# Seven block products for eight in the gate and up projections of a float32 encoder layer

## The chip, the cores and the metric

The kernel runs on one core of one Trainium2 chip. The metric is the device time of one execution in microseconds (us), from the start of the program to its end. TensorE (PE in the profile) multiplies, VectorE (DVE) and ScalarE (ACT) do the elementwise work, SyncE (SP) issues the transfers, and each engine works through its own queue in order.

## The reference

One layer of an encoder on 512 tokens of 1024 features, float32, in four sublayers, each with an RMSNorm before and after it:

```python
def swiglu(x, w_gate, w_up, w_down):
    return (jax.nn.silu(x @ w_gate) * (x @ w_up)) @ w_down

f = swiglu(rms_norm(h, ffn1_pre_g[i]), ffn1_w_gate[i], ffn1_w_up[i], ffn1_w_down[i])
h = h + 0.5 * rms_norm(f, ffn1_post_g[i])
m = hybrid_mixer(rms_norm(h, mix_pre_g[i]), ...)
h = h + rms_norm(m, mix_post_g[i])
f = swiglu(rms_norm(h, ffn2_pre_g[i]), ffn2_w_gate[i], ffn2_w_up[i], ffn2_w_down[i])
h = h + 0.5 * rms_norm(f, ffn2_post_g[i])
e = (p[i] @ ple_w_proj[i]) * jax.nn.sigmoid(rms_norm(h, ple_pre_g[i]) @ ple_w_gate[i])
h = h + rms_norm(e, ple_post_g[i])
```

`w_gate` and `w_up` are 1024 x 2816, `w_down` is 2816 x 1024, so each of the two feed-forward sublayers (FFN) has 22 tiles of 128 hidden features.

## The kernel before

Features lie on the 128 partitions and tokens along the free axis. An activation of 1024 features is eight tiles `[128, 512]`. Each product is made in float32r from values split in two parts (high and low), by three matmuls: `mm3` (L227) multiplies weight-high by x-high (L228), weight-high by x-low (L229) and weight-low by x-high (L230). The weights are the stationary side, the tokens the moving side, so one matmul has a 128x128 weight tile and 512 columns (256 where the tokens are taken in halves).

The weights come as a stream of chunks `[128, 1024]` of 512 KB (class `Stream`, L167). `load` issues a chunk's transfer from SP into one of `NRAW` = 2 buffers `raw`. `pump` splits it: ACT writes the high part `whi` (L195), DVE subtracts and writes the low part `wlo` (L196, seen as L160, the helper `tt`). There are `NB` = 8 buffers of each, and `free` pumps `SPLIT_AHEAD` = 4 chunks ahead of the one that was used up.

In an FFN the 11 groups of hidden tiles (two gate tiles and two up tiles each) stand in three parts, groups 0 to 2, 3 to 6 and 7 to 10. `group` (L344) makes one group from four chunks: 8 input tiles x 4 output tiles x 3 = 96 matmuls of 512 columns into four PSUM banks. The evacuation `ev_gu` (L418) multiplies the gate by the tokens' norm factor `rb`, applies SiLU on ACT, multiplies by the up product and splits the result into `zh` and `zl`. `rb` is left out of the up product: the factor that is missing in a token of f is taken care of by the norm after the FFN, with `scaled` (L272). After each part come the down products of its groups in two output halves.

The order of the instructions is made by emission: `Clock` (L65) advances with each product emitted, and tasks (norms, residual updates, splits) are emitted between products at distances given in the table `TIMES`; within that order the framework's scheduler places each engine's queue. At the end of a sublayer `last_group` (L369) takes the last products by halves of the tokens, `ahead` (L387) splits the chunks that the next sublayer begins with, as many as the `NB` buffers hold, and `boundary` (L395) does the norms, the residual and the next input's split. `first_group` (L352) then takes the next sublayer's first four chunks, by halves of the tokens.

Of the kernel before, what the change touches and what calls it, by code (L numbers as in the profile page):

```python
# [27 lines left out]
NB = 8  # L28
NRAW = 2
SPLIT_AHEAD = 4  # L30
# Where steps go between the products: distances on the emission clock, by sublayer boundary, head pair or channel group.
# [14 lines left out]
    "out": 3.8,  # L46
    "held": 2,
# [6 lines left out]
class Task:  # L54
    """Work emitted in steps: a generator that yields how long (us of products) to wait before its next step."""
# [7 lines left out]
class Clock:  # L63
    """Orders the emission: time advances with the products emitted, and due steps of tasks go between them."""
# [35 lines left out]
    def need(self, t, steps=None):  # L100
        """Emits what is left of a task, or of its first steps."""
# [13 lines left out]
def kernel(  # L115
# [13 lines left out]
    wraw = ctx.enter_context(tc.tile_pool(name="wraw", bufs=NRAW))  # L129
    wsp = ctx.enter_context(tc.tile_pool(name="wsp", bufs=NB))  # L130
# [35 lines left out]
    class Stream:  # L166
        def __init__(self):  # L167
            self.loaded = 0
            self.split = 0
            self.done = 0  # L170
            self.hold = False
            self.freed = set()
            self.raw = {}
            self.parts = {}

        def load(self, upto):
            while self.loaded < min(upto, n_chunks):
# [5 lines left out]
                self.loaded += 1  # L183

        def pump(self, upto):
            while self.split < min(upto, self.done + NB, n_chunks):
                c = self.split
                self.load(c + 1)
                raw = self.raw.pop(c)
# [3 lines left out]
                for i in range(0, CH, w):  # L193
                    sl = slice(i, i + w)
                    nc.scalar.copy(hi[:, sl], raw[:, sl])  # L195
                    tt(lo[:, sl], raw[:, sl], f32(hi[:, sl]), ALU.subtract)  # L196
                self.parts[c] = (hi, lo)
                self.split += 1
                self.load(self.split + NRAW)
# [54 lines left out]
    veps = act.tile([P, NT], F32, name="veps")  # L254
# [17 lines left out]
    def norm(sl, rc, wait, scaled=False):  # L272
# [11 lines left out]
        if scaled:  # L284
            for b in range(nb):
                nc.scalar.activation(sd[:, b:b + 1], ps[:, b:b + 1], AF.Sqrt, bias=veps[:, b0 + b:b0 + b + 1],
                                     scale=1.0 / D)
        else:
            nc.scalar.activation(sd[:, :nb], ps[:, :nb], AF.Sqrt, bias=eps, scale=1.0 / D)
        if rc is not None:  # L290
            nc.vector.tensor_scalar(veps[:, b0:b0 + nb], ps[:, :nb], EPS / D, EPS * EPS, op0=ALU.mult, op1=ALU.add)
# [16 lines left out]
    def emit_group(c0, nch, rhs, ps, sl, free, evac=None, before=None):  # L308
        """All output tiles together, k outermost; with evac, one output tile after the other."""
# [8 lines left out]
        if evac is None:  # L318
            for c in range(nch):
                for kk in range(2):  # L320
                    if before:
                        before(2 * c + kk)
                    for t in range(4):
                        one(c, kk, t)
                if free:
# [11 lines left out]
    def half_banks():  # L337
        """Four accumulators of 256 columns in two banks; the first product of a bank opens both."""
# [5 lines left out]
    def group(c0, nch, rhs, evac, late=()):  # L344
        ps = [bank("g") for _ in range(4)]
        emit_group(c0, nch, rhs, ps, slice(0, S), True)
# [5 lines left out]
    def first_group(c0, rhs, evac, chains):  # L352
        """The first products of a sublayer, by halves of the tokens, as its input comes."""
# [15 lines left out]
    def last_group(c0, nch, rhs, evac, chain):  # L369
        """The last products of a sublayer, by halves of the tokens; returns the tasks that follow each."""  # L370
# [16 lines left out]
    def ahead():  # L387
        """Splits of the chunks that the next sublayer begins with."""
        upto = min(ws.done + NB, n_chunks)
# [5 lines left out]
    def boundary(f, gpost, gnext, scaled):  # L395
        def chain(sl, i):
            yield from norm(sl, None, at("nb", i), scaled)
# [13 lines left out]
    def ffn(chains, gpost, gnext):  # L411
        f = [None] * KD
        late = ()
        for pi, (g0, g1) in enumerate(PARTS):
# [3 lines left out]
            def ev_gu(t, ps, sl, j0, held={}):  # L418
                if t % 2 == 0:
                    g = ttile("t")  # L420
                    tt(g[:, sl], ps, rb[:, sl], ALU.mult)
                    nc.scalar.activation(g[:, sl], g[:, sl], AF.Silu)  # L422
# [3 lines left out]
                if j not in zh:  # L426
                    zh[j], zl[j] = ztile(j)
                v = vtile("v")
                tt(v[:, sl], ps, g[:, sl], ALU.mult)
                nc.scalar.copy(zh[j][:, sl], v[:, sl])  # L430
# [554 lines left out]
```

## Time and profile before

| what | value |
|---|---|
| runs: median (lowest, highest) of 3 | 1114.62 us (1113.77, 1114.8) |
| profiled execution, first to last instruction | 1111.1 us |
| what lies around the span, by the median | 3.5 us |
| PE busy in the span | 1094.0 us (98%) |
| DVE busy, ACT busy | 578.6 us (52%), 454.1 us (41%) |
| traffic over the span | 96 GB/s |

A row of a view names the line in the kernel, the engine, the operation and the tiles: `wlo<-raw,whi` reads `raw` and `whi` and writes `wlo`. Matmuls overlap in the array, so the length of one in a row (0.39 us) is more than the distance between two starts; the distance is what counts.

### The profile page before, as it was taken

Reading aid. Unit: us, or ns where it says so; the run is one execution under the profiler, and the core shown is the slowest. Engines: PE = TensorE matmul, PEld = TensorE weight load, DVE = VectorE, ACT = ScalarE, POOL = GpSimd, SP = SyncE. Lnnn points to the kernel's source line nnn. Section 1 sums busy time; section 2 is a strip of 40 time slices with the busy share of each in tenths; the row PEclk is TensorE's granted clock in tenths of the full one; section 3 lists DMA queues with packets and bytes.
Section 4 is the critical chain, followed back from the end, with each engine's and each line's share of the span. In section 5 each row is a group of like instructions: output and inputs, shape, how many; then the busy total and the mean of one; then the engine's idle time right before and its main releaser. Section 6 shows DMA issues by size and latency. Waiting matters only on the chain.

```text
span 1111.1 us, 14120 instructions
## 1 busy us (share of the span) xinstructions
PE 1094.0 (98%) x5610; PEld 930.1 (84%) x5610; DVE 578.6 (52%) x1041; ACT 454.1 (41%) x765; POOL 0.7 (0%) x6
## 2 busy tenths in 40 slices
PE   9999999999999999999999999999999999999995
PEld 7888888888889988887888899888888888889994
DVE  6642334333434987977444439632334333434976
ACT  7533223212323665366232257523223212323784
POOL 0000000000000000000000000000000000000000
PEclk9999999999999999999999999999999999999998
DMA  6553222232332043231223210533232222332112
GB/s 221 184 162 118 95 95 95 95 94 95 97 97 73 20 133 114 76 95 59 95 95 95 95 58 31 176 117 96 95 95 95 94 95 95 97 99 72 38 58 76
DMA packets 37010, 107.94 MB, mean 97 GB/s; under 512 B 4816, under 2 KB 11472, under 8 KB 36944
## 3 DMA queue, kind: packets, MB, share of 16 engines
q1 hardware_dynamic: 36800, 107.01, 29.8%
q8 instruction: 44, 0.72, 0.3%
q14 instruction: 22, 0.18, 0.1%
q10 hardware_dynamic: 144, 0.03, 0.0%
HBM read 104.93 MB, written 2.10 MB: 96 GB/s over the span
## 4 chain that ended last, share of the span: by engine, by line
PE 94%; DVE 2%; ACT 2%; issue 1%; DMA 0%; SPq 0%; DVEq 0%; ACTq 0%
PE g L228 25%; PE g L230 25%; PE g L229 25%; PE gate L228 2%; PE gate L229 2%; PE gate L230 2%; PE br L228 1%; PE br L230 1%; PE br L229 1%; DVE o L160 1%; ACT e L567 1%; PE v L229 1%; PE xp L228 1%; PE v L228 1%; PE v L230 1%; PE xp L230 1%
## 5 line engine op out<-in xcount | busy, mean ns | idle before, releaser
L160 DVE TENSOR_TENSOR wlo<-raw,whi 128x1024 fp32r<-128x1024 f32 (+1 forms) x195 | 235.3, 1208 | 340.8 <-ACT whi L195 340.2
L195 ACT CAST whi<-raw 128x1024 fp32r<-128x1024 f32 (+1 forms) x195 | 202.1, 1038 | 422.6 <-PE g L229 301.1
L228 PE MATMUL g<-uh,whi 128*128 128x512 f32 (+1 forms) x960 | 345.9, 362 | 0.4 <-ACT whi L195 0.4
L229 PE MATMUL g<-ul,whi 128*128 128x512 f32 (+1 forms) x960 | 346.3, 361 | 0.0
L230 PE MATMUL g<-uh,wlo 128*128 128x512 f32 (+1 forms) x960 | 345.7, 361 | 0.5 <-DVE wlo L160 0.5
L230 PEld LDWEIGHTS g<-uh,wlo 128*128 128x128 f32 x960 | 180.7, 188 | 28.6 <-DVE wlo L160 0.9
L228 PEld LDWEIGHTS g<-uh,whi 128*128 128x128 f32 x960 | 180.7, 188 | 28.3 <-ACT whi L195 0.9
L229 PEld LDWEIGHTS g<-ul,whi 128*128 128x128 f32 x960 | 180.8, 188 | 27.5 <-DVE ul L163 0.2
L228 PE MATMUL g<-zh,whi 128*128 128x512 f32 (+1 forms) x512 | 179.9, 351 | 0.0
L230 PE MATMUL g<-zh,wlo 128*128 128x512 f32 (+1 forms) x512 | 179.0, 350 | 0.0
L229 PE MATMUL g<-zl,whi 128*128 128x512 f32 (+1 forms) x512 | 177.9, 347 | 0.0
L230 PEld LDWEIGHTS g<-zh,wlo 128*128 128x128 f32 x512 | 96.0, 188 | 14.1
L229 PEld LDWEIGHTS g<-zl,whi 128*128 128x128 f32 x512 | 96.1, 188 | 13.6
L228 PEld LDWEIGHTS g<-zh,whi 128*128 128x128 f32 x512 | 96.3, 188 | 12.1
L160 DVE TENSOR_TENSOR acc<-acc,sq 128x256 f32<-128x256 f32 (+1 forms) x96 | 44.7, 466 | 17.9 <-ACT sq L269 16.7
L422 ACT ACTIVATE t<-t 128x512 f32<-128x512 f32 (+1 forms) x46 | 27.9, 610 | 63.5 <-DVE t L160 63.4
L160 DVE TENSOR_TENSOR t<-g,rb 128x512 f32<-128x512 f32 (+1 forms) x46 | 30.5, 667 | 39.6 <-PE g L230 38.4
L228 PE MATMUL gate<-uh,whi 128*128 128x512 f32 x128 | 50.6, 395 | 0.0
L230 PE MATMUL gate<-uh,wlo 128*128 128x512 f32 x128 | 50.0, 390 | 0.0
L229 PE MATMUL gate<-ul,whi 128*128 128x512 f32 x128 | 49.9, 390 | 0.0
L430 ACT CAST zh<-v 128x512 fp32r<-128x512 f32 (+1 forms) x46 | 27.3, 596 | 27.9 <-DVE v L160 27.8
L160 DVE TENSOR_TENSOR zl<-v,zh 128x512 fp32r<-128x512 f32 (+1 forms) x46 | 30.5, 665 | 13.1 <-ACT zh L430 13.1
(150 smaller groups left out, 960.8 us busy)
## 6 DMA issues: line engine op xcount, KB each, us to landing
raw<-in_wst SPq DMA_DIRECT2D x191, 512.0 KB, 3.4
h<-in_x SPq DMA_DIRECT2D x8, 256.0 KB, 5.7
bm<-in_bias SPq DMA_DIRECT2D x64, 32.0 KB, 3.3
out<-o SPq DMA_DIRECT2D x16, 128.0 KB, 1.7
raw<-in_wst SPq DMA_DIRECT2D x4, 128.0 KB, 3.5
g_sb<-in_gains ACTq DMA_DIRECT2D x1, 34.0 KB, 3.0
edge_sb<-in_edge SPq DMA_DIRECT2D x1, 32.0 KB, 5.9
```

The costliest lines, as they stand in the source:

```text
L160: nc.vector.tensor_tensor(o, a, b, op=op)
L195: nc.scalar.copy(hi[:, sl], raw[:, sl])
L228: nc.tensor.matmul(o, wh, xh, start=first, stop=False, **kw)
L229: nc.tensor.matmul(o, wh, xl, start=False, stop=False, **kw)
L230: nc.tensor.matmul(o, wl, xh, start=False, stop=last, **kw)
L422: nc.scalar.activation(g[:, sl], g[:, sl], AF.Silu)
L430: nc.scalar.copy(zh[j][:, sl], v[:, sl])
L567: nc.scalar.activation(e[:, ii, :], e[:, ii, :], AF.Exp, bias=mn[:, ii:ii + 1], scale=-1.0, accum_out=sm[:, ii:ii + 1])
```

## The change

In each FFN the groups 3 to 10 (16 of the 22 pairs of tiles) are made by a scheme of seven block products in place of eight. A group is a product of two by two blocks: the outputs are halved into gate and up (two tiles each), the 1024 features into two halves, the tokens into two halves. Seven products of such blocks, some of sums of weight blocks with sums of input blocks, give the four output blocks. One product has 2 output tiles x 4 feature tiles x 3 = 24 matmuls of 256 columns, a group 168 in place of 96 of 512 columns. The seven are added up in three PSUM banks p, q, r; ACT copies three intermediate sums out (m1, m16, m7), and DVE makes three of the output blocks from these and a bank.

What goes with it:

- `Stream` has operations in place of chunks: four chunks of a fast group give seven splits. Four sums of weight blocks are made on DVE before (`both`, and in place in `raw`). `NRAW` is 5, `NB` is 6.
- The inputs have to be normalized before they are summed: `normalized` makes `un` = gain x h x rb, `renew` splits it into `uh`, `ul` again during group 1, `combined` makes the sums of blocks and splits them into eight pairs of tiles x. Groups 0 and 1 still use the input without `rb`, and their evacuation multiplies a second time by `rb`. The norm after the FFN loses `scaled`.
- The tiles x take buffers (tag `y`) of the mixer's bias tiles `bm`, so the 64 transfers of the bias wait until x has been used in the first FFN; before they stood among the first 40 us of weight loads and later ones.

```diff
-NB = 8
-NRAW = 2
+FAST = range(3, 11)
+NB = 6
+NRAW = 5
+RAW_AHEAD = 2
...
+        def source(self, n):
+            kind, c, i = self.ops[n]
+            if not kind:
+                return self.raw[c], (c,)
+            a21, a22, a11, a12 = (self.raw.get(c + j) for j in range(4))
+            if i == 2:
+                self.both = wsum.tile([P, CH], F32, tag="sum", name="both")
+                tt(self.both, a21, a22, ALU.add)
+                tt(a21, a21, a11, ALU.add)
+                tt(a11, a11, self.both, ALU.add)
+            if i == 6:
+                tt(a12, a12, a11, ALU.add)
...
+        def product(i, o, first):
+            wh, wl = ws.get(c0 + i)
+            for t in range(2):
+                for kk in range(4):
+                    w = slice((kk * 2 + t) * P, (kk * 2 + t + 1) * P)
+                    xh, xl = moving(i, kk)
+                    mm3(o[:, t * 256:(t + 1) * 256], wh[:, w], wl[:, w], xh, xl,
+                        first and kk == 0 and t == 0, kk == 3, skip_group_check=True)
+            ws.free(c0 + i)
...
+        product(0, p, True)
+        m1 = kept("m1", p)
+        product(1, q, True)
+        made(0, 0, q, m1, ALU.add)
+        product(2, p, False)
+        m16 = kept("m16", p, acc)
+        product(3, r, True)
+        m7 = kept("m7", r)
+        product(4, p, False)
+        made(1, 1, m7, p, ALU.subtract)
+        product(5, r, False)
+        made(1, 0, r, m16, ALU.subtract)
+        product(6, p, False)
+        done(0, 1, p, True)
...
+            def fast(gi):
+                j0 = 2 * (gi - g0)
+                v = {}
+                def block(row, column, c, banked):
+                    if row not in v:
+                        v[row] = vtile("v")
+                    g = ttile("g")[:, LEFT] if banked else c[:, LEFT]
+                    nc.scalar.activation(g, c[:, LEFT], AF.Silu)
+                    tt(v[row][:, HALVES[column]], c[:, RIGHT], g, ALU.mult)
+                    if (row, column) in ((1, 0), (0, 1)):
+                        split_z(j0 + row, v[row], slice(0, S))
+                fast_group(take(7), moving, block)
```

DVE's queue in the second FFN part of the first FFN, before, over group 4 of the kernel (`t`, `v` and `zl` are the evacuation, a number behind `wlo` is the chunk):

```order
L160 TENSOR_TENSOR wlo26_1045<-raw26_966,whi26_1044 128x1024
L160 TENSOR_TENSOR wlo27_1075<-raw27_996,whi27_1074 128x1024
L160 TENSOR_TENSOR wlo28_1105<-raw28_1048,whi28_1104 128x1024
L160 TENSOR_TENSOR t_998<-g_874,rb_105 128x512
L160 TENSOR_TENSOR t_1007<-g_876,rb_105 128x512
L160 TENSOR_TENSOR v_1003<-g_875,t_998 128x512
L160 TENSOR_TENSOR wlo29_1135<-raw29_1078,whi29_1134 128x1024
L160 TENSOR_TENSOR zl_1002<-v_1003,zh_1001 128x512
L160 TENSOR_TENSOR v_1012<-g_877,t_1007 128x512
L160 TENSOR_TENSOR zl_1011<-v_1012,zh_1010 128x512
```

The same engine and part now (`w` are output blocks made from a bank, `raw` and `both` on the left are weight sums, the number behind `wlo` is the split):

```order
L165 TENSOR_TENSOR raw26_1088<-raw26_1088,raw28_1322 128x1024
L165 TENSOR_TENSOR wlo31_1294<-raw25_1086,whi31_1293 128x1024
L165 TENSOR_TENSOR w_1263<-q_1203,m1_1233 128x512
L165 TENSOR_TENSOR wlo32_1325<-raw28_1322,whi32_1324 128x1024
L165 TENSOR_TENSOR v_1265<-w_1263 128x256
L165 TENSOR_TENSOR raw28_1322<-raw28_1322,both_1391 128x1024
L165 TENSOR_TENSOR wlo33_1359<-raw29_1328,whi33_1358 128x1024
L165 TENSOR_TENSOR raw29_1328<-raw29_1328,raw28_1322 128x1024
L165 TENSOR_TENSOR wlo34_1396<-raw28_1322,whi34_1395 128x1024
L165 TENSOR_TENSOR w_1362<-m7_1332,p_1202 128x512
L165 TENSOR_TENSOR wlo35_1432<-raw26_1088,whi35_1431 128x1024
L165 TENSOR_TENSOR v_1364<-w_1362 128x256
```

The evacuation no longer stands in one piece behind the group: its steps stand between the splits and the sums for the group after it.

ACT's queue at that place, before:

```order
L195 CAST whi28_1104<-raw28_1048 128x1024
L422 ACTIVATE t_998<-t_998 128x512
L195 CAST whi29_1134<-raw29_1078 128x1024
L422 ACTIVATE t_1007<-t_1007 128x512
L430 CAST zh_1001<-v_1003 128x512
L430 CAST zh_1010<-v_1012 128x512
L195 CAST whi30_1186<-raw30_1108 128x1024
```

And now, over the first five of the seven products of one group:

```order
L470 COPY m1_1233<-p_1202 128x512
L239 CAST whi32_1324<-raw28_1322 128x1024
L577 ACTIVATE w_1263<-w_1263 128x256
L239 CAST whi33_1358<-raw29_1328 128x1024
L470 COPY acc_107<-p_1202 128x512
L239 CAST whi34_1395<-raw28_1322 128x1024
L470 COPY m7_1332<-r_1204 128x512
L239 CAST whi35_1431<-raw26_1088 128x1024
```

Between two copies out of a bank now stands a cast for a later group, and once a SiLU that reads what DVE made.

PE's queue around the end of group 0 of the first FFN, before (`nsum` and `nb` are the sums and the broadcast of the norm):

```order
L303 MATMUL nb_318<-dh_300,ones_r_76 128x256
L281 MATMUL nsum_322<-ones_75,acc_104 128x1 x2
L229 MATMUL g_188<-ul6_102,whi3_178 128x512
L230 MATMUL g_188<-uh6_94,wlo3_179 128x512
...
L304 MATMUL nb_318<-dl_301,ones_r_76 128x256
L228 MATMUL g_186<-uh7_95,whi3_178 128x512
...
L303 MATMUL nb_344<-dh_329,ones_r_76 128x256
```

And now:

```order
L336 MATMUL nb_319<-dh_301,ones_r_79 128x256
L321 MATMUL nsum_323<-ones_78,acc_107 128x1 x2
L273 MATMUL g_191<-uh7_98,whi3_180 128x512
L274 MATMUL g_191<-ul7_106,whi3_180 128x512
L275 MATMUL g_191<-uh7_98,wlo3_181 128x512
L337 MATMUL nb_319<-dl_302,ones_r_79 128x256
L336 MATMUL nb_344<-dh_329,ones_r_79 128x256
L273 MATMUL g_394<-uh0_91,whi4_216 128x512
```

The six products that stood between the last `nb` matmul of the first token half and the first of the second half stand ahead of both now.

## Rows read from the trace of the kernel before

**Rows 1.** The page: busy time by engine, and the chain that ended last

```profile
PE 1094.0 (98%) x5610; PEld 930.1 (84%) x5610; DVE 578.6 (52%) x1041; ACT 454.1 (41%) x765; POOL 0.7 (0%) x6
...
PE 94%; DVE 2%; ACT 2%; issue 1%; DMA 0%; SPq 0%; DVEq 0%; ACTq 0%
```

**Rows 2.** Busy time by stretch: two FFN parts, a last group, a first group

```profile
core 0: us, PE busy (x) PEld busy (x) DVE busy (x) ACT busy (x) POOL busy (x), PEclk, DMA share, GB/s
105.64:192.73 87.09, 87.09 (x386) 72.07 (x384) 32.40 (x36) 24.90 (x32) 0.00 (x0) 1.00 0.30 97
...
903.38:990.47 87.09, 87.09 (x385) 72.07 (x384) 33.30 (x38) 24.40 (x30) 0.00 (x0) 1.00 0.30 97
...
345.77:369.03 23.26, 23.26 (x200) 23.19 (x198) 13.25 (x32) 9.97 (x22) 0.00 (x0) 1.00 0.07 24
...
670.16:695.54 25.38, 25.18 (x211) 24.94 (x209) 24.96 (x67) 19.23 (x47) 0.00 (x0) 1.00 0.13 43
```

**Rows 3.** Timeline of PE: start, length, instruction; 512 columns, then 256

```profile
60.20 0.39 PE L230 MATMUL g<-uh,wlo 128*128 128x512 f32 x1
60.42 0.39 PE L228 MATMUL g<-uh,whi 128*128 128x512 f32 x1
...
355.19 0.28 PE L230 MATMUL g<-zh,wlo 128*128 128x256 f32 x1
355.31 0.28 PE L228 MATMUL g<-zh,whi 128*128 128x256 f32 x1
...
381.69 0.28 PE L228 MATMUL g<-uh,whi 128*128 128x256 f32 x1
381.81 0.28 PE L229 MATMUL g<-ul,whi 128*128 128x256 f32 x1
```

**Rows 4.** Groups of DVE's instructions by form: busy, mean ns, idle before, releaser

```profile
L160 DVE TENSOR_TENSOR wlo<-raw,whi 128x1024 fp32r<-128x1024 f32 x191 | 233.7, 1224 | 340.7 <-ACT whi L195 340.2
...
L160 DVE TENSOR_TENSOR zl<-v,zh 128x512 fp32r<-128x512 f32 x42 | 28.9, 688 | 13.1 <-ACT zh L430 13.1
```

**Rows 5.** Timeline of DVE where instructions stand back to back

```profile
347.18 1.22 DVE L160 TENSOR_TENSOR wlo<-raw,whi 128x1024 fp32r<-128x1024 f32 x1
348.31 0.69 DVE L160 TENSOR_TENSOR acc<-acc,sq 128x512 f32<-128x512 f32 x1
348.91 0.42 DVE L160 TENSOR_TENSOR f<-g,f 128x256 f32<-128x256 f32 x1
349.25 0.68 DVE L160 TENSOR_TENSOR acc<-acc,sq 128x512 f32<-128x512 f32 x1
```

**Rows 6.** Groups of ACT's instructions by form

```profile
L195 ACT CAST whi<-raw 128x1024 fp32r<-128x1024 f32 x191 | 200.5, 1051 | 422.5 <-PE g L229 301.1 <-PE gate L229 42.9 <-PE br L229 28.0
...
L430 ACT CAST zh<-v 128x512 fp32r<-128x512 f32 x42 | 25.8, 614 | 27.9 <-DVE v L160 27.8
...
L455 ACT COPY f<-g 128x512 f32<-128x512 f32 x16 | 9.4, 585 | 11.1 <-PE g L230 10.3
...
L793 ACT ACTIVATE g<-g 128x256 f32<-128x256 f32 x16 | 6.4, 411 | 4.2 <-DVE g L160 4.2
```

**Rows 7.** The page, issues of transfers: count, KB each, us to landing

```profile
raw<-in_wst SPq DMA_DIRECT2D x191, 512.0 KB, 3.4
```

**Rows 8.** Timeline, ACT between the two norm broadcasts at the start

```profile
26.33 0.37 ACT L305 COPY rb<-nb 128x256 f32<-128x256 f32 x1 [0.19 <-PE nb L304]
26.59 0.70 ACT L299 ACTIVATE dh<-ident,rc_pre 128x128 fp32r<-128x128 f32 x2
```

**Rows 9.** Timeline, DVE and PE where first groups of a sublayer begin

```profile
374.77 0.16 DVE L294 RECIPROCAL rc<-sd 128x2 f32<-128x2 f32 x1
...
1047.45 0.28 PE L228 MATMUL g<-uh,whi 128*128 128x256 f32 x1
...
1050.97 0.48 DVE L163 SCALAR_TENSOR_TENSOR h<-t,gh,h 128x256 f32<-128x256 f32 x1
...
1053.58 0.48 DVE L163 SCALAR_TENSOR_TENSOR ul<-h,g_sb,uh 128x256 fp32r<-128x256 f32 x1
```

More of the change, by code (lines that the diff above doesn't have):

```diff
@@ L166 @@
     class Stream:
+        LOADS = (3, 4, 4, 4, 4, 4, 4)
         def __init__(self):
+            self.ops = []
+            self.needs = []
+            chunk = 0
+            for kind in plan():
+                for i in range(7 if kind else 1):
+                    self.ops.append((kind, chunk, i))
+                    self.needs.append(chunk + (self.LOADS[i] if kind else 1))
+                chunk += 4 if kind else 1
+            self.n = len(self.ops)
+            assert chunk == n_chunks
             self.loaded = 0
@@ L172, in __init__ @@
             self.freed = set()
+            self.over = set()
             self.raw = {}
             self.parts = {}
+            self.both = None
         def load(self, upto):
-            while self.loaded < min(upto, n_chunks):
+            while self.loaded < min(upto, n_chunks) and (self.loaded < NRAW or self.loaded - NRAW in self.over):
                 c = self.loaded
@@ L183, in load, with drop @@
                 self.loaded += 1
+        def drop(self, *chunks):
+            for c in chunks:
+                del self.raw[c]
+                self.over.add(c)
+        def source(self, n):
[10 more added lines that the diff above has]
+                tt(a12, a12, a11, ALU.add)
+            return ((a11, ()), (a12, ()), (a11, ()), (a21, (c,)), (self.both, ()), (a22, (c + 1,)),
+                    (a12, (c + 2, c + 3)))[i]
         def pump(self, upto):
-            while self.split < min(upto, self.done + NB, n_chunks):
+            while self.split < min(upto, self.done + NB, self.n):
                 c = self.split
-                self.load(c + 1)
-                raw = self.raw.pop(c)
+                self.load(self.needs[c])
+                assert self.loaded >= self.needs[c]
+                raw, over = self.source(c)
                 hi = wsp.tile([P, CH], F32R, tag="whi", name=f"whi{c}")
@@ L196, in pump @@
                     tt(lo[:, sl], raw[:, sl], f32(hi[:, sl]), ALU.subtract)
+                self.drop(*over)
                 self.parts[c] = (hi, lo)
                 self.split += 1
-                self.load(self.split + NRAW)
+                self.load(self.needs[c] + RAW_AHEAD)
         def get(self, c):
@@ L270, in add_square, with norm @@
             tt(acc[:, sl], acc[:, sl], sq[:, sl], ALU.add)
-    def norm(sl, rc, wait, scaled=False):
+    def norm(sl, rc, wait):
         b0, nb = sl.start // P, (sl.stop - sl.start) // P
@@ L283, in norm @@
         sd = tmp.tile([P, NT], F32, tag="sd", name="sd")
[L284 to L291, printed above, removed]
+        nc.scalar.activation(sd[:, :nb], ps[:, :nb], AF.Sqrt, bias=eps, scale=1.0 / D)
         if rc is None:
@@ L305, in norm, with emit_group @@
         nc.scalar.copy(rb[:, sl], pb[:, :nb * P])
-    def emit_group(c0, nch, rhs, ps, sl, free, evac=None, before=None):
+    def emit_group(c0, nch, rhs, ps, sl, free, evac=None, before=None, after=None):
         def one(c, kk, t):
@@ L408, in boundary, with fast_group, kept, made @@
         return chain
-    def ffn(chains, gpost, gnext):
+    LEFT, RIGHT = HALVES
+    def fast_group(c0, moving, done):
+        p, q, r = (bank(n) for n in "pqr")
+        def product(i, o, first):
[7 more added lines that the diff above has]
+            ws.free(c0 + i)
+        def kept(name, o, tile=None):
+            k = wide(name, "sq")[:, 0:S] if tile is None else tile
+            nc.scalar.copy(k, o)
+            return k
+        def made(row, column, a, b, op):
+            w = ttile("w")
+            tt(w, a, b, op)
+            done(row, column, w, False)
+        product(0, p, True)
[12 more added lines that the diff above has]
+        done(0, 1, p, True)
@@ L882, in _stationary, with plan, _quad @@
     return a.transpose(0, 2, 1, 3, 4).reshape(k // 2, P, CH)
+def plan():
+    ffn = []
+    for g0, g1 in PARTS:
+        for g in range(g0, g1):
+            ffn += [True] if g in FAST else [False] * 4
+        ffn += [False] * (2 * (g1 - g0))
+    mixer = [False] * (4 * 4 + 1 + 16 + 8 + 8)
+    return ffn + mixer + ffn + [False] * (1 + 2 + 8)
+def _quad(w, pairs):
+    out = []
+    for i, j in ((1, 0), (1, 1), (0, 0), (0, 1)):
+        a = np.stack([w[j * 512:(j + 1) * 512, pair[i]:pair[i] + P] for pair in pairs], 1)
+        out.append(a.reshape(4, P, 2, P).transpose(1, 0, 2, 3).reshape(1, P, CH))
+    return np.concatenate(out, 0)
 def _ffn_chunks(wg, wu, wd):
@@ L891, in _ffn_chunks @@
             j = 2 * g * P
-            out.append(_stationary(both, [j, F + j, j + P, F + j + P]))
+            if g in FAST:
+                out.append(_quad(both, [(j, j + P), (F + j, F + j + P)]))
+            else:
+                out.append(_stationary(both, [j, F + j, j + P, F + j + P]))
         rows = wd[2 * g0 * P:2 * g1 * P]
```

98 lines of the change are left out of this document (77 added, 21 removed).

## The prediction

> **What bounds the kernel now.** I read the page first: PE is busy for 98% of the span, and 94% of the chain that ended last is PE's [rows 1]. Then the busy time by stretch. The four stretches in which the change works (groups 3 to 6 and 7 to 10 of both FFNs; the first and the last stand in the rows) take 87.09 us each and PE is busy for all of it, DVE for 32.4 to 33.3 and ACT for some 25, at a full granted clock of 1.00 [rows 2]. So nothing is waited for there but PE, and a shorter PE time is a shorter kernel for as long as DVE and ACT, whose work grows, keep up. What DVE and ACT do before is wait: 340.2 us of DVE's idle time ahead of `wlo` is ACT's cast, and 301.1 of ACT's ahead of `whi` is PE giving back a buffer [rows 4, 6].
>
> **PE's part.** A stretch has 4 groups x 96 = 384 matmuls, 87.09 / 384 = 226.8 ns each, 21.77 us a group. Now a group has 168 of 256 columns. Their distance is read where the kernel already uses 256 columns: 0.12 us between two starts, in a last group and in a first group [rows 3]. Over longer runs without a norm between, I count 0.118 us where the tokens come from `zh`, `zl` and 0.120 where they come from `uh`, `ul`. Three of the seven products read `uh`, `ul` and four the new tiles x; I take 0.119. A group is then 168 x 0.119 = 19.99 us, one product of 24 matmuls 2.86 us, and a group gives back 21.77 - 19.99 = 1.78 us; 16 groups give 28.5 us. By 0.118 it would be 31.2, by 0.120 25.8; I keep both for the range. PE has no other new work: the rest of its matmuls are the same ones.
>
> Against this speaks a rule of the Trainium skill, in "TensorE: Matmul & The Clock Gate", section "Back-to-back issue gap": the spacing of matmuls is set by the weight load as well as by the columns, and it gives 81 ns at 128 columns and 131 ns at 512. Drawn as a line that is an estimate of 98 ns at 256, a group of 16.4 us against 12.6, so the change would cost 61 us. The trace does not agree: its 226.8 and 119 ns leave a fixed part of 2 x 119 - 226.8 = 11 ns.
>
> **DVE and ACT in a fast group.** DVE has 7 splits and 4 sums of 1024 columns, 3 output blocks and 2 `zl` of 512, 4 products `v` of 256. The trace has no sum of two `raw`; the nearest row is `wlo`, also 1024 columns from two tiles, 1224 ns [rows 4]. Back to back the distances are 1.13 us for 1024 columns, 0.60 for 512 and 0.34 for 256 [rows 5]: 11 x 1.13 + 5 x 0.60 + 4 x 0.34 = 16.8 us. With whole durations (1.224, 0.688, 0.42) it is 13.5 + 3.4 + 1.7 = 18.6. Either is below 19.99, but DVE goes from 37% busy to 84 or 93%. ACT has 7 x 1.05 + 3 x 0.585 + 4 x 0.41 + 2 x 0.61 = 12.0 us [rows 6], 60%.
>
> A sum does not settle it, since both queues are in order and now hold steps that wait for PE. So I put one group's steps behind each other, in the order in which they stand, with time 0 at the end of PE's product 1, product ends every 2.86 us, and a split's buffer free six products after it was taken. DVE: block from q 0 to 0.7, split 0 of the next group to 2.3 (its cast runs 0 to 1.05), `v`, a sum to 3.7, split 1 (its buffer is free at 2.86) to 5.1, a sum to 6.2, split 2 to 7.9; then it idles until product 4 ends at 8.6. Block, split 3, `v` to 11.2; product 5 ends at 11.4; block, split 4, `v`, the sum `both`, `zl`, `v`, split 5, `zl`, a sum and split 6 follow without a gap to 20.1. The next block may start at 20.0. So DVE is just in time at the tightest place and has 0.7 us of waiting ahead of the third product and 0.2 ahead of product 5 even if late; by whole durations it comes 0.5 late there and makes it up.
>
> PE waits for none of that directly. What it waits for are banks: m1 copied before product 2, m16 before product 4, m7 before product 5, the block from p before product 6. In the same list the copies end 1.2 us before they are needed and the block 2.2 us before. The splits are ready 12 us before their products. The four loads of a group wait for splits of the group before, 3.4 us each [rows 7]; each has 2.1 to 3.5 us more than that until it is read. So I cost DVE, ACT and loads in the 16 groups at nothing, under the cover of PE; if the cover of 1.2 us at the copies goes, the rivals below say the price.
>
> **What else moves.** Preparing x (8 `un`, 8 renewed `ul`, 16 block sums, 8 splits, some 21 us on DVE, and a second multiplication by `rb`) lies in groups 1 and 2, 43 us of PE work, and is needed at group 3; those tiles are needed one group after they can be made, so I cost it at nothing. Four places are not covered:
>
> - Start. PE's queue now has the second norm broadcast right behind the first, and ACT between them a cast, the copy of `rb` and two `dh`: 1.05 + 0.37 + 0.70 [rows 6, 8], of which some 0.1 overlaps PE. PE stands for 2.0 us.
> - First FFN to mixer. With `NB` 6 only two of the first group's four chunks can be split ahead. The third's `wlo` now stands behind the reciprocal, at 374.77 [rows 9], and ends at 376.1; PE wants it at 369.03 [rows 2] + 48 x 0.12 + 0.5 for a norm sum + 0.24 = 375.5. With one more split ahead of the second token half's chain I take 1.1 us.
> - Mixer to second FFN: the same shift, some slack: 0.3 us.
> - Second FFN to the embedding. The second chunk of the first group now stands behind the residual step that started at 1050.97, ending at about 1052.6, and PE, starting at 1047.45 [rows 9], wants it after 2 x 1.44 + 0.24, at 1050.6 to 1051.2. The third stands behind `ul` of 1053.58 and the split before it, ending at 1056.3, against 1055.5. I take 2.5 us.
>
> Together 5.9 us; nothing at the least, since the scheduler chose these places, and 12 at the most (twice my waits). The later bias transfers hold SP for 64 x some 0.6 us while PE has over 40 us of split and loaded chunks and products ahead: nothing.
>
> **Sum.** The profiled execution spans 1111.1 us, the median of the runs is 3.5 above; that part stays. 1111.1 - 28.5 + 5.9 + 3.5 = 1092.0 us.
>
> **Rivals.**
>
> 1. DVE becomes the bound of the fast groups. For it: 93% by whole durations. Against it: the chain above has room. If in addition each `v` waited out its SiLU (4 x 0.41) and each `zl` its cast (2 x 0.61) the group would take 18.6 + 1.6 + 1.2 = 21.4, giving back 0.37 x 16 = 5.9: 1114.6 - 5.9 + 5.9 = 1114.6. Half way there, 20.7 us a group, gives 1103. This rival lies between 1099 and 1114.
> 2. Slower: the banks. Each of four hand-backs in a group has 1.2 us of cover. If ACT runs one step late, a copy stands behind a cast and a SiLU (1.05 + 0.41), ends 2.05 us after its product instead of early, and PE waits 0.85 us four times, 3.4 us a group, 54 in all: 1146. The break-even is at (28.5 - 5.9) / 64 = 0.35 us a hand-back, when copies come 1.6 us later than in my list. For it: ACT's casts wait for PE and its SiLUs for DVE, in one queue.
> 3. Slower: the pace of 256 columns. The weight loads fill 23.19 of 23.26 us in the last group [rows 2], so they may set the pace. A whole first group runs at 25.38 / 192 = 132.2 ns with norms and waits in it [rows 2]; at that pace a group is 22.2, 7 us lost: 1127. It decides from 127.4 ns. Against it: no run without norms is above 120. The skill's rule above is this rival's mechanism.
>
> That the change does not do what it says I give nothing: PE's queue holds 16 x 168 matmuls of 256 columns in place of 16 x 96 of 512.
>
> **Chances.** Forecast, 1084 to 1099: 0.70. Rival 1: 0.19, three in four of it faster by over 0.2% (2.2 us, about what a measurement of this kernel tells from no change). Rival 2: 0.08. Rival 3: 0.03. That makes faster 0.85, same 0.05, slower 0.10. The range runs from 31.2 us of gain and no stalls, 1084 (rounded), to rival 1 a little past its middle, 1107.
>
> **What would show it.** The distance of matmuls in the fast groups at 118 to 120 ns; their four stretches near 80 us instead of 87.09; DVE busy for 67 to 75 us in each; no PE wait for `m` copies or blocks; new PE waits of 1 to 3 us at the start and before the embedding. Wrong would be: PE waiting for `wlo` or ACT's copies within a fast group (rivals 1, 2), or more than 121 ns between matmuls (rival 3).

## The result, and the profile after

The changed kernel takes 1094.88 us (median of 4 runs, 1093.59 to 1095.4) where the kernel before takes 1114.3 beside it: a ratio of 0.9827, 95% interval 0.9813 to 0.9841. The forecast was 1092.0. All times are medians of runs in the fast state; one run of `a_pad32` below, 1625.45 us at a granted clock of 0.66, was in the slow state and is not counted. The profiled execution spans 1091.8 us against 1111.1, so 19.3 us are gone; the prediction's sum for the span was 1111.1 - 28.5 + 5.9 = 1088.5.

The page of the kernel after, the lines that answer to [rows 1]:

```profile
PE 1071.5 (98%) x6762; PEld 961.3 (88%) x6762; DVE 763.4 (70%) x1279; ACT 543.2 (50%) x921; POOL 0.7 (0%) x6
...
PE 91%; DVE 5%; ACT 3%; issue 1%; DMA 0%; SPq 0%; DVEq 0%; ACTq 0%
```

PE still bounds the kernel, but DVE and ACT now hold 8% of the chain. Busy time by stretch of the kernel after (the columns are those of [rows 2]): the first down products, two of the four fast stretches, and the first group of the second FFN:

```profile
74.29:107.89 33.60, 33.60 (x145) 26.99 (x144) 15.29 (x15) 11.38 (x16) 0.00 (x0) 1.00 0.16 51
107.89:187.84 79.95, 79.95 (x673) 79.95 (x672) 62.60 (x71) 43.73 (x64) 0.00 (x0) 1.00 0.39 119
889.72:969.67 79.95, 79.95 (x674) 79.94 (x673) 64.14 (x74) 43.23 (x62) 0.00 (x0) 1.00 0.38 119
661.23:687.44 26.21, 25.21 (x211) 24.83 (x209) 25.58 (x67) 21.06 (x49) 0.00 (x0) 1.00 0.19 61
```

The fast stretches take 79.95 us where 87.09 stood in [rows 2]: 672 matmuls at 79.95 / 672 = 119.0 ns, and no idle time of PE. The down products in the first row are not touched by the diff, yet they took less before:

```profile
72.66:105.64 32.98, 32.98 (x146) 27.04 (x144) 10.06 (x11) 11.78 (x16) 0.00 (x0) 1.00 0.42 123
```

PE is busy without a gap in both, at a full granted clock, with the same 144 matmuls: 229.0 ns each before, 233.3 now. Cut at the first matmul of each stage, the two spans differ like this:

| stage | before | after | difference |
|---|---|---|---|
| up to the first matmul | 4.82 | 4.97 | +0.15 |
| groups 0 to 2, first FFN | 67.84 | 69.32 | +1.48 |
| four fast stretches | 348.36 | 319.80 | -28.56 |
| six stretches of down products, 512 columns | 197.86 | 201.60 | +3.74 |
| three last groups, 256 columns | 69.86 | 69.54 | -0.32 |
| mixer up to its output product | 255.85 | 257.39 | +1.54 |
| output product, 512 columns | 21.98 | 22.40 | +0.42 |
| first group of the second FFN | 25.38 | 26.21 | +0.83 |
| groups 1 and 2 of the second FFN, projection of the embedding | 55.50 | 55.66 | +0.16 |
| embedding to the end | 63.65 | 64.91 | +1.26 |

So the fast groups gave what was forecast to a tenth of a microsecond. Of the 9.3 us that went the other way about half are new waits at the starts of stages, and half are stages whose matmuls only became slower.

Inside a fast group each bank comes back about where the prediction's list put it. ACT, DVE and PE in the second fast group, the copies and the block, and the first matmul of the product that needs the bank back:

```profile
131.79 0.58 ACT L470 COPY m<-p 128x512 f32<-128x512 f32 x1
133.64 0.28 PE L273 MATMUL p<-x,whi 128*128 128x256 f32 x1
...
140.36 0.58 ACT L470 COPY m<-r 128x512 f32<-128x512 f32 x1
142.12 0.28 PE L273 MATMUL r<-x,whi 128*128 128x256 f32 x1
...
142.39 0.69 DVE L165 TENSOR_TENSOR w<-m,p 128x512 f32<-128x512 f32 x1 [0.68 <-PE p L275]
145.00 0.28 PE L273 MATMUL p<-uh,whi 128*128 128x256 f32 x1
```

m1 is out at 132.37, 1.27 us before PE writes p again; m7 at 140.94, 1.18 before PE needs r; the block from p at 143.08, 1.92 before product 6. The prediction had 1.2 and 2.2. Over all 16 groups the trace has 1.14 to 1.27 us for the copies (once 0.94) and 1.92 for the block (once 1.57). DVE waited 0.68 us ahead of that block, as listed (0.7). The two largest of DVE's waits in the first fast stretch, of 17.35 us idle (in all, times, longest):

```profile
DVE wlo L165 <- ACT whi L239: 11.6, 24, 1.8
DVE w L165 <- PE p L275: 2.7, 4, 0.7
```

### The profile page after: what moved, and what is told of

It is laid out like the page before. It is cut to its first block, busy times and chain, and to the rows that moved or that the text cites. A ratio compares the mean times of both kernels' runs of the same rounds, so it can differ in the third digit from the quotient of the medians.

```text
span 1091.8 us, 16876 instructions
## 1 busy us (share of the span) xinstructions
PE 1071.5 (98%) x6762; PEld 961.3 (88%) x6762; DVE 763.4 (70%) x1279; ACT 543.2 (50%) x921; POOL 0.7 (0%) x6
## 4 chain that ended last, share of the span: by engine, by line
PE 91%; DVE 5%; ACT 3%; issue 1%; DMA 0%; SPq 0%; DVEq 0%; ACTq 0%
PE g L275 15%; PE g L273 15%; PE g L274 15%; PE p L274 6%; PE p L275 6%; PE p L273 6%; PE r L274 3%; PE r L275 3%; PE r L273 3%; PE gate L273 2%; PE gate L274 2%; PE gate L275 2%; PE q L275 1%; PE q L274 1%; PE q L273 1%; PE br L273 1%
## 5 line engine op out<-in xcount | busy, mean ns | idle before, releaser
L275 PE MATMUL g<-uh,wlo 128*128 128x256 f32 (+1 forms) x448 | 146.3, 330 | 1.0 <-DVE wlo L165 0.9
L274 PE MATMUL g<-ul,whi 128*128 128x256 f32 (+1 forms) x448 | 147.0, 329 | 0.0
L273 PE MATMUL g<-uh,whi 128*128 128x256 f32 (+1 forms) x448 | 146.0, 330 | 0.6 <-ACT whi L239 0.6
L275 PEld LDWEIGHTS g<-uh,wlo 128*128 128x128 f32 x448 | 84.7, 190 | 9.0 <-DVE wlo L165 1.5
L273 PEld LDWEIGHTS g<-uh,whi 128*128 128x128 f32 x448 | 84.7, 190 | 8.4 <-ACT whi L239 0.9
L274 PEld LDWEIGHTS g<-ul,whi 128*128 128x128 f32 x448 | 84.9, 190 | 8.1 <-DVE ul L168 0.6
L274 PE MATMUL p<-ul,whi 128*128 128x256 f32 x256 | 72.4, 283 | 0.0
L275 PE MATMUL p<-uh,wlo 128*128 128x256 f32 x256 | 72.4, 283 | 0.0
L273 PE MATMUL p<-uh,whi 128*128 128x256 f32 x256 | 72.4, 283 | 0.0
L274 PE MATMUL p<-x,whi 128*128 128x256 f32 x256 | 72.0, 281 | 0.0
L273 PE MATMUL p<-x,whi 128*128 128x256 f32 x256 | 71.6, 280 | 0.0
```

The costliest lines, as they stand in the source:

```text
L273: nc.tensor.matmul(o, wh, xh, start=first, stop=False, **kw)
L274: nc.tensor.matmul(o, wh, xl, start=False, stop=False, **kw)
L275: nc.tensor.matmul(o, wl, xh, start=False, stop=last, **kw)
```

## The experiments

The ratio to the kernel before, run beside each, is given where it decides. The first 75 us of two traces of like kernels differ by up to 2 us, so what follows is read from stretches behind that.

### Where the tiles lie: four kernels with a pad

The diff removes `veps`, a tile that took up 32 bytes per partition and that the norm with `scaled` used. It stood ahead of zh and zl, so these and the later tiles of their pool moved down by 32 bytes. First theory (A): the place of the moving tile sets the time between its matmuls. Rival (B): busier engines beside PE, or fewer weight buffers. The edit, with 8 or 24 floats in the changed kernel and 16 or 24 in the one before:

```diff
     rc_pre = act.tile([P, NT], F32, name="rc_pre")
+    pad = act.tile([P, 8], F32, name="pad")
+    nc.vector.memset(pad, 0.0)
```

> The changed kernel with 32 bytes of unused SBUF per partition put back where the tile `veps` stood, so that zh, zl, x and all later tiles move up by 32 bytes, to where zh and zl lay before (64 bytes past a multiple of 128). Theory A: the distance of the down projections' matmuls went from 229 to 233.3 ns because their moving tiles lie 32 bytes past a multiple of 128; then it returns to 229 ns here, the first down stretch from 33.60 to 32.98 us, and the kernel gains (0.62 + 0.84 + 0.41) x 2 + 0.42 + 0.8 = 5 us: 1089.9. Theory B: the distance grew because DVE and ACT are busier beside PE, or because there are six weight buffers in place of eight; then 33.60 us stays and the time is 1094.9.

> The changed kernel with 96 bytes put in at the same place, so that zh, zl, x, the mixer's y and o lie on multiples of 128 as uh and ul do. Theory A, if the position alone decides: z at 512 columns goes to the 226.8 ns of uh and ul (first down stretch 32.66 us), z at 256 columns and x from 117 to 118 to the 120 ns of uh and ul, so a fast stretch goes from 79.95 to 672 x 0.120 = 80.64. Gain some 1150 x 6.5 ns = 7.5 us at 512 columns, loss 4 x 0.7 + 3 x 0.5 = 4.3 at 256: 1091.7. Theory B: no change, 1094.9.

> The kernel before with 96 bytes put in ahead of zh, so that zh and zl lie 32 bytes past a multiple of 128, as in the changed kernel, with nothing else changed. Theory A: 233.3 ns, the first down stretch 33.60 us in place of 32.98, and the kernel is 5 us slower: 1119.5. Theory B: no change, 1114.5.

> The kernel before with 64 bytes put in ahead of zh, so that zh and zl lie on multiples of 128. Theory A: 226.8 ns, the first down stretch 32.66 us in place of 32.98, some 1150 x 2.2 ns = 2.5 us faster, less 3 x 0.5 us where z is read by 256 columns: 1113.4. Theory B: no change, 1114.5.

Measured: 1092.25, 1091.94, 1119.98 and 1118.48 us. The kernel before, with nothing but a pad, became slower, by 0.54% (1.0037 to 1.0071) and 0.41% (1.0026 to 1.0056). Its first down products with 96 bytes:

```profile
73.78:107.50 33.72, 33.72 (x145) 27.12 (x144) 10.05 (x11) 11.77 (x16) 0.00 (x0) 1.00 0.39 121
```

33.72 us in place of 32.98, with DVE and ACT as idle as before and eight weight buffers. So the place alone can do it, without B. But theory A as it was put falls: with 64 bytes, zh on a multiple of 128 like uh, this stretch took 33.59, not 32.66. (The changed kernel with 96 bytes came within 0.3 us of theory A's 1091.7 by luck: its first down products stayed at 33.60, and its first fast stretch became shorter, 79.23, where the theory had it longer.) And with 32 bytes the changed kernel got back only part. Its first and its second down products, behind 512-column groups and behind a fast stretch:

```profile
74.96:107.94 32.98, 32.98 (x146) 27.04 (x144) 15.46 (x15) 11.40 (x16) 0.00 (x0) 1.00 0.15 52
187.87:232.67 44.80, 44.80 (x195) 36.29 (x193) 22.12 (x23) 9.65 (x11) 0.00 (x0) 1.00 0.22 71
```

The first is back at 229.0 ns, the second (192 matmuls) stays at 233.3, though the tiles lie the same. So the place matters, 128 is not its measure, and at this place either pace can hold.

### Where the tiles lie: aligned with the weights

By the addresses in the built programs, in the kernel before, the changed one and all four with pads, uh, ul and all weight tiles lie 256 bytes past a multiple of 512; zh and zl were 32, 64, 128 or 160 bytes off that. Theory A2: what counts is the distance between moving and weight tile modulo 512. The same edit with 480 bytes in the changed kernel and 448 in the one before brings it to 0:

> The changed kernel with 480 unused bytes put in ahead of un, zh, zl and x, so that zh, zl, the mixer's y and o, and the first four pairs of x lie at the same place within 512 bytes as the weight tiles whi and wlo do (0 apart; in the runs with pads they were 32, 64, 128 and 160 bytes apart, and only uh and ul were 0 apart). Theory A2, that the distance between moving and weight tile modulo 512 bytes sets the pace: z at 512 columns takes the 227 ns of uh and ul (first down stretch 32.7 us in place of 33.60), some 1150 x 6.3 ns = 7.2 us faster; at 256 columns z and the first four x take 120 ns in place of 117 to 118.5: the first two fast stretches get up to 1 us longer each. Together some 1091. Theory A, position modulo 128 alone: as with 96 bytes of pad, down stretch 33.5, 1091.9, and no fast stretch longer. If neither, the down stretch stays at 33.6.

> The kernel before with 448 unused bytes put in ahead of zh, so that its zh and zl too lie 0 apart from the weight tiles modulo 512 bytes. Theory A2: z at 512 columns from 229 to 227 ns, first down stretch from 32.98 to 32.65 us, 864 x 2.2 ns in the down products and w_out's and the branches' 288 x 2.2, 2.5 us in all, less 576 x 2 ns where z is read by 256 columns (118 to 120): 1112.5. Beside the changed kernel with 480 bytes it gives the change without its shift of the tiles: 1112.5 - 1090.6 = 22, which is 28.5 less the stalls of some 5.

Measured: 1090.61 us (0.979 of the kernel before) and 1111.59 (0.9982, 0.9973 to 0.9991). The first down products and the first fast stretch of the changed kernel with 480 bytes, then the first down products of the kernel before with 448:

```profile
75.89:108.53 32.64, 32.64 (x145) 27.04 (x144) 15.25 (x15) 11.34 (x16) 0.00 (x0) 1.00 0.19 56
108.53:188.79 80.26, 80.26 (x673) 80.25 (x672) 62.49 (x71) 43.81 (x64) 0.00 (x0) 1.00 0.39 119
```

```profile
73.39:106.03 32.64, 32.64 (x146) 27.03 (x144) 10.05 (x11) 11.77 (x16) 0.00 (x0) 1.00 0.42 124
```

Both come to 32.64 us, and to 226.7 to 227.0 ns a matmul in every down stretch. The one has six buffer pairs and busy engines, the other eight and idle ones, so nothing is left for theory B here. The fast stretches are 0.3 us longer, since half of x now lies at distance 0 too, where 256 columns cost more. With both kernels so placed the change is worth 1111.59 - 1090.61 = 21.0 us, against 19.4 as it came (the two ran on different chips, where the kernel before took 1113.38 and 1113.95 us).

### Distance or place, and a faster kernel

At 256 columns the traces so far had 120 ns at distance 0 and less at others, least for the x tiles at 448 bytes. `best1` uses both: z at 0, x at 448; and it splits one chunk fewer ahead during the first group.

```diff
-                self.pump(max(self.done, c + 1) + SPLIT_AHEAD)
+                self.pump(max(self.done, c + 1) + (3 if c < 4 else SPLIT_AHEAD))
...
+    pad = act.tile([P, 120], F32, name="pad")
...
+            if n < 4:
+                apart(act, 112, "pad_y")
+            elif n < 6:
+                apart(tmp, 32, "pad_t")
```

(`apart` makes a pad of so many floats in a pool, once; a third of 16 floats behind the tag `y` brings the later zh and zl back to 0.) `best1_shift` moves weights, u, z and x together by 32 bytes, with a pad among the constants.

> The changed kernel with the places of its tiles chosen: 480 bytes ahead of un, zh, zl as in the run before, and all eight pairs of x 448 bytes apart from the weights modulo 512 (where single x tiles of an earlier run took 113 to 116 ns), and with only three splits ahead while the first group runs, so that the two norm broadcasts of the start stand apart. By the place: fast stretches from 80.3 us to 4 x 168 x (3 x 0.120 + 4 x 0.1145) / 7 = 78.5, 7 us in all; by the start, 1.6 us less: 1090.6 - 7 - 1.6 = 1082. If the 113 to 116 ns belonged to those tiles' products and not to their place, the fast stretches stay at 80 and it is 1089. The mixer's y comes to lie 448 apart too, which is unknown at 512 columns: up to 1.4 us more.

> The kernel best1 with 32 unused bytes put in ahead of everything but the constants, so that weights, uh, ul, zh, zl and x all move up by 32 bytes and keep their distances from each other. If the distance between the moving tile and the weight tile modulo 512 bytes sets the pace: the same time, 1080, down stretch 32.64 us, fast stretch 78.08. If the place of the moving tile by itself does (in all runs so far the weights lay at the same place, 256 bytes past a multiple of 512): z and u at 512 columns go to the 233.3 ns of a place 32 bytes off, the first down stretch to 33.6 us, the groups 0 to 2 and the mixer slower as well, some 3000 x 6 ns = 18 us in all, 1098, and the fast stretches change too.

Measured: 1080.13 us (0.9699, 0.9685 to 0.9712) and 1079.35 (0.9693, 0.9677 to 0.9709). Down products and fast stretch of `best1`:

```profile
73.71:106.35 32.64, 32.64 (x145) 27.03 (x144) 15.18 (x14) 11.27 (x16) 0.00 (x0) 1.00 0.17 54
106.35:184.43 78.08, 78.08 (x674) 78.07 (x673) 62.58 (x71) 43.73 (x64) 0.00 (x0) 1.00 0.38 122
```

Its timeline of PE in a product from uh (distance 0) and one from x (448):

```profile
109.83 0.28 PE L276 MATMUL q<-uh,wlo 128*128 128x256 f32 x1
...
110.78 0.28 PE L275 MATMUL q<-ul,whi 128*128 128x256 f32 x1
...
112.23 0.28 PE L275 MATMUL p<-x,whi 128*128 128x256 f32 x1
...
113.94 0.28 PE L275 MATMUL p<-x,whi 128*128 128x256 f32 x1
```

8 steps in 0.95 us are 119 ns, 15 steps in 1.71 us 114 ns. With everything shifted by 32 bytes (`best1_shift`) the same two stretches stay as they were:

```profile
73.09:105.73 32.64, 32.64 (x146) 27.04 (x144) 15.18 (x14) 11.27 (x16) 0.00 (x0) 1.00 0.17 54
105.73:183.80 78.07, 78.07 (x673) 78.07 (x672) 62.60 (x71) 43.72 (x64) 0.00 (x0) 1.00 0.40 122
```

So, as far as one shift shows, it is the distance between the two tiles that counts, not where either lies. Of the gain over 1090.61 the fast stretches carry 4 x 2.18 = 8.7 us. The mixer's y, which came to lie at 448 too, costs 0.7 us in the branch products (43.59 to 44.33). PE had no wait between the two norm broadcasts of the start any more.

### How much cover DVE gives

Two kernels repeat one weight sum, three times (`sums6`) or five times (`sums8`, the edit shown; the result stays):

```diff
-                tt(self.both, a21, a22, ALU.add)
+                for _ in range(5):
+                    tt(self.both, a21, a22, ALU.add)
```

> The changed kernel with the first weight sum of each fast group made three times instead of once (same result), two more DVE instructions of 1024 columns, 2 x 1.13 = 2.3 us a group; DVE then has 15.65 + 2.3 = 17.9 us of work in a group in which PE has 19.99. Forecast's view (DVE is cover as long as its work is below PE's, since its waits can be filled): stretches stay at 79.95 us, 1094.9. Rival 1 (the waits of its in-order queue, 4.3 us a group in the trace, stay whatever it has to do): 15.65 + 2.3 + 4.3 = 22.2 us a group, 2.2 x 16 = 35 us slower, 1130.

> The same with that sum made five times: DVE has 15.65 + 4 x 1.13 = 20.2 us of work a group, just over PE's 19.99, by whole durations of 1.22 us 20.5. Forecast's view: DVE becomes the bound, and by no more than its work, 0.2 to 0.5 us a group, 3 to 8 us in all, 1098 to 1103. Rival 1, with the waits of the queue kept: 20.2 + 4.3 = 24.5 us a group, 72 us slower, 1167.

Measured: 1094.02 and 1094.68 us, 0.9824 and 0.9831 of the kernel before, where the changed kernel had 0.9827: no change for either. The first fast stretch with five sums, and DVE's largest wait in it:

```profile
108.74:188.69 79.95, 79.95 (x674) 79.95 (x673) 73.85 (x83) 43.93 (x64) 0.00 (x0) 1.00 0.39 119
```

```profile
DVE wlo L165 <- ACT whi L240: 3.7, 8, 1.6
```

DVE is busy for 73.85 of 79.95 us, and its waits for ACT's casts went from 11.6 to 3.7 us: they are not a fixed price of the in-order queue but slack that more work fills. Rival 1 falls. So does my 3 to 8 us: I charged each of the four groups of a stretch with its own splits and sums, but those of a stretch's first group are mostly done during the down products ahead of it. The stretch got 12 more DVE instructions, not 16.

### How much cover the banks have

The three copies out of a bank are made four times in a row:

```diff
-            nc.scalar.copy(k, o)
+            for _ in range(4):
+                nc.scalar.copy(k, o)
```

> The changed kernel with each of the three copies out of a bank (m1, m16, m7) made four times in a row into the same tile: three more ACT copies of some 0.5 us, so the bank is given back 1.5 to 1.7 us later, and ACT has 10.9 + 9 x 0.55 = 16 us of work a group, below 19.99. Forecast's and rival 2's price of a hand-back: the cover in the trace is 1.14 to 1.27 us, so PE waits 0.3 to 0.5 us at each of three products, 0.9 to 1.5 us a group, 14 to 24 us in all: 1109 to 1119. If ACT's idle share alone counted: no change, 1094.9.

Measured: 1104.49 us (0.9916, 0.99 to 0.9933), 9.6 more than the changed kernel, where 14 to 24 was expected and no change by ACT's idle share. The first fast stretch, and ACT in it:

```profile
109.87:193.64 83.77, 83.52 (x680) 81.51 (x678) 61.97 (x71) 62.12 (x100) 0.00 (x0) 1.00 0.37 114
```

```profile
142.26 0.57 ACT L471 COPY acc<-p 128x512 f32<-128x512 f32 x1
142.74 0.59 ACT L471 COPY m<-r 128x512 f32<-128x512 f32 x1
143.21 0.60 ACT L471 COPY acc<-p 128x512 f32<-128x512 f32 x1
...
145.12 0.64 ACT L471 COPY acc<-p 128x512 f32<-128x512 f32 x1
```

And PE, where it needs p back:

```profile
145.50 0.28 PE L273 MATMUL q<-uh,whi 128*128 128x256 f32 x1
145.81 0.39 PE L273 MATMUL p<-x,whi 128*128 128x256 f32 x1
146.03 0.28 PE L274 MATMUL p<-x,whi 128*128 128x256 f32 x1
```

The fourth copy of m16 ends at 145.76. PE's matmul into p starts at 145.81, 0.31 us after the one ahead of it, and the next 0.22 us later, in place of 0.12 each. Eight products of this stretch start so, which costs some 2.3 us in it. ACT is busy for 62 of 84 us and PE is nevertheless late: the cover of rival 2 is real and ends where ACT still has a quarter of its time free. The price is lower than I worked out because the framework's scheduler answered the longer copies: copies of two banks alternate, and in PE's queue pieces of other products stand where the wait would have been, eight matmuls of the down products among them. 9.6 us over 48 copies are 0.2 us each.

### What six buffer pairs cost at the starts of stages

```diff
-NB = 6
+NB = 5
```

> The changed kernel with five pairs of weight buffers in place of six (the tiles keep their places modulo 512). If the new waits at the starts of the mixer, the second FFN and the embedding come from fewer chunks split ahead, as the prediction has it, each grows by about one split more, 1.2 to 1.5 us: 3 to 5 us slower, 1098 to 1100, with the fast stretches at 79.95 (a split's buffer comes free one product later, with 12 us to spare). If they come from the norm chain alone: no change, 1094.9. If the fast groups are nearer to the edge than the prediction says, their stretches grow.

Measured: 1100.64 us, 5.8 more (6.6 by the ratios to the kernel before, 0.9886 and 0.9827). The fast stretch stays at 79.95. PE's waits for the low part of a split in the whole run, after (one wait) and with five pairs:

```profile
PE g L275 <- DVE wlo L165: 0.9, 1, 0.9
```

```profile
PE g L275 <- DVE wlo L165: 5.6, 4, 2.9
```

By stages the mixer got 1.4 us longer, the first group of the second FFN 3.3, the embedding with its projection 3.5; the start, where the two broadcasts stand apart in this kernel, 1.6 shorter (the profiled spans differ by 6.7). So fewer splits ahead do cost waits at these places, in two of the three by more than one split (1.22 us). That the changed kernel's own waits come from six pairs in place of eight is argued from this: no run has the change with eight.

## Why the prediction held, and where it did not

**PE's part** was right: 168 x 119 ns a group, 28.56 us measured against 28.5. The Trainium skill's rule weighed there, TensorE: Matmul & The Clock Gate, section "Back-to-back issue gap", would have made it a loss by an estimate of 98 ns at 256 columns. The traces do not agree: no run has a mean below 113 ns for any of its tiles. That the pace came out at 119.0 is in part luck: of the x tiles, which the trace of before could not show, one half ran at 117 ns and the other at 120, and with other places of x a stretch took 78.07 to 80.26 us, a gain of 36 or 27 us.

**"PE has no other new work: the rest of its matmuls are the same ones"** is the step that failed. They are the same instructions, but a 32-byte tile fewer moved their operands, and z at 512 columns went from 229.0 to 233.3 ns: 3.74 us in the down products, 0.42 in the mixer's output product, and 0.72 in its branch products (44.09 to 44.81 us, start to start in the trace), 4.9 in all. The diff showed it, in the line where `veps` goes; no row of before did, since all its z lay at one distance. Two paces for one shape stood in the trace of before (226.8 for u and 229.0 for z at 512 columns, 120 and 118 at 256), and I took a mean instead of asking why.

**DVE, ACT and loads at nothing** was right, and for the reason given: PE has no wait in any fast stretch, and the cover of 1.2 and 2.2 us was measured as 1.14 to 1.27 (once 0.94) and 1.92 (once 1.57). The bound for the sum of two `raw` was good (1224 ns taken, 1222 measured). DVE's 67 to 75 us a stretch were too many (62.5 to 64.2), because a stretch holds the splits and sums of some three of its groups, 71 to 74 instructions against the 80 that I counted.

**What else moves**, 5.9 us: measured some 4.4. The start cost 1.5 of the 2.0, read from the stretch in which two traces can differ by as much. PE in the kernel after, at the broadcast that answers to [rows 8]:

```profile
30.35 0.39 PE L336 MATMUL nb<-dh,ones_r 128*128 128x256 f32 x1 [1.70 <-ACT dh L332]
```

The wait is as worked out, but a wait of 0.5 us for `wlo` that stood in the first group before is gone.

First FFN to mixer, 1.1: 1.54, less the 0.72 of the slower branch products, 0.8. The size is near, the cause is not the one I gave: PE waits for no `wlo` in this first group. Its matmuls stand up to 0.3 us apart in place of 0.12 where `uh` and `ul` of the second token half come late from ACT and DVE:

```profile
373.55 0.49 ACT L305 ACTIVATE uh<-h,g_sb 128x256 fp32r<-128x256 f32 x1
374.08 0.48 DVE L168 SCALAR_TENSOR_TENSOR ul<-h,g_sb,uh 128x256 fp32r<-128x256 f32 x1 [0.23 <-ACT uh L305]
374.10 0.50 PE L273 MATMUL g<-uh,whi 128*128 128x256 f32 x2
374.62 0.39 PE L274 MATMUL g<-ul,whi 128*128 128x256 f32 x1
```

Mixer to second FFN, 0.3: 0.83, too small. PE waits there for the last of the norm's sums on DVE, not for a split, so the place was another than the shift that I named; why DVE comes later there than before, no run separates:

```profile
687.00 0.58 PE L321 MATMUL nsum<-ones,acc 128*128 128x1 f32 x4 [0.73 <-DVE acc L165]
```

Second FFN to the embedding, 2.5: 1.26. There the mechanism is the one described, at another chunk and smaller. DVE and PE at that place:

```profile
1030.15 0.48 DVE L168 SCALAR_TENSOR_TENSOR h<-t,gh,h 128x256 f32<-128x256 f32 x1
1030.54 1.22 DVE L165 TENSOR_TENSOR wlo<-raw,whi 128x1024 fp32r<-128x1024 f32 x1
...
1031.81 0.50 PE L275 MATMUL g<-uh,wlo 128*128 128x256 f32 x2 [0.93 <-DVE wlo L165]
```

One `wlo` stands behind a residual step and PE waits 0.93 us for it; the second wait that I had added did not come, since everything after it was already shifted by the first. So of the four places two had the wait that I named and two another one: that their sum is near is in part luck.

**The rivals.** Rival 1: DVE has at least 11 us of room in a stretch (`sums8`). Rival 2 exists as a mechanism, with a cover of 1.2 us and a lower price than I gave it (`copies4`). Rival 3 did not happen: 119.0 ns on the mean, though the pace of 256 columns is not one number either (113 to 120).

**The sum.** 28.56 gained, some 4.4 lost in new waits, 4.9 in slower matmuls: 19.3. The waits came out 1.5 us below the 5.9 and hid part of the missing term, by luck, so the forecast was 3 us too low and not 5.

## What to carry to other kernels

Where PE bounds a stage, cutting its columns paid in full here as long as the other engines' steps ended before PE asked for them: list one period of the queues and read the smallest cover, since a sum of busy time neither shows that cover nor its end. After any edit that adds or drops a tile, look at the time between matmuls in stages that the edit doesn't touch: here one pad of 480 bytes took the changed kernel from 1094.88 to 1090.61 us, and four pads of 64 to 480 bytes, with one split fewer ahead at the start, took it to 1080.13. Price what a larger buffer demand takes from the look-ahead at stage borders, where DVE is full.

## What was not expected of the hardware

**The distance between moving and weight tile changes the pace of matmuls**, at a full granted clock and without idle time. By the distance modulo 512 bytes per partition, from the first down products (144 matmuls of 512 columns):

| distance | stretch, us | ns a matmul | kernels |
|---|---|---|---|
| 0 | 32.64 | 226.7 | 480 and 448 bytes of pad, `best1`, `best1_shift` |
| 32 | 33.60 | 233.3 | after |
| 64 | 32.98 | 229.0 | before, 32 bytes of pad |
| 128 | 33.59, 33.60 | 233.3 | 64 and 96 bytes of pad |
| 160 | 33.72 | 234.2 | before with 96 bytes of pad |

At 512 columns distance 0 is the fastest of these; at 256 columns it is the slowest, by little: 120 ns, against 117 at 32, 118 at 64 and 320, 119 at 128, 160 and 384, 120 at 352 and 114 at 448 (means from start to start, z and x of all these kernels). That the period is 512 bytes is not shown: 64 with 320 and 128 with 384 ran alike, so 256 would fit as well; 128 would not, since 0 and 128 differ. The Trainium skill, TensorE: Matmul & The Clock Gate, section "Step-by-step: what each phase is for", says that loading the next tile's weights takes no read bandwidth from the running matmul, because each has its own port. By that the pace should not depend on where the two tiles lie. The runs show 3% at 512 columns and 5% at 256 that come and go with their distance, so here the measurement decides; whether it is the weight load that takes the time, no run shows. Why the distance matters, and why at distance 64 the second down products of the padded changed kernel stay at 233.3 ns while the first run at 229.0, stays open; that those 233.3 follow a fast stretch is all that the traces show.

**A short wait can cost more than itself.** With five buffer pairs, PE in the first group of the second FFN, and the granted clock (the column before the last two) behind it:

```profile
666.70 0.79 PE L275 MATMUL g<-uh,wlo 128*128 128x256 f32 x2 [1.08 <-DVE wlo L165]
...
667.50 0.41 PE L274 MATMUL g<-ul,whi 128*128 128x256 f32 x1
667.72 0.41 PE L275 MATMUL g<-uh,wlo 128*128 128x256 f32 x1
...
670.22 0.28 PE L274 MATMUL g<-ul,whi 128*128 128x256 f32 x1
670.34 0.28 PE L275 MATMUL g<-uh,wlo 128*128 128x256 f32 x1
```

```profile
667.40:669.00 1.60, 1.60 (x10) 1.60 (x9) 1.60 (x4) 0.55 (x2) 0.00 (x0) 0.50 0.77 210
```

After waits of 0.27 us (at 664.43) and 1.08 us (at 666.70) PE ran at a granted clock of 0.50, the lower level of 1.2 GHz, with 0.21 us between matmuls, until about 670.1. From 666.70 to 670.1 at 0.21 in place of 0.12 us a matmul is some 1.4 us: more than the wait. That is part of why five pairs cost more than one split a stage. In the kernel after, the wait of 0.93 us in the embedding's first group left the clock at 1.00; what decides between the two, no run here shows.
